# Windowed attention in an encoder layer: scores and attended values as three fp32r products of high and low parts, in place of plain fp32 products

## The chip, the core and the metric

The kernel runs on one core of a Trainium2 chip. The metric is the device time of one execution, in microseconds (us). The engines carry short names in the profile: PE is TensorE (PEld its weight loads), DVE is VectorE, ACT is ScalarE, POOL is GpSimd, and SP is SyncE, which issues most of the DMAs.

## What is computed

One encoder layer over 256 tokens of width 2048: a SwiGLU feed-forward block, a mixer with two groups of heads beside each other, and a second SwiGLU block, each between RMS norms. The mixer projects the tokens once, to 6656 columns; 5120 of them feed eight heads of a bidirectional gated recurrence (HGRN2), the other 1536 feed windowed attention with eight query heads and two key/value heads of width 128. Of the reference, the attention is what matters here (shortened; with 256 tokens every query block sees both key blocks):

```python
def window_attention(q, k, v, sink, rel_table):
    scores = jnp.einsum('bncxgd,bnsxd->bxgncs', qb, kb).astype(jnp.float32) / math.sqrt(ATTN_HEAD_DIM)
    bias = rel_table.astype(jnp.float32)[t5_buckets(rel)]
    scores = jnp.where(valid, scores + bias, NEG_INF)
    probs = jax.nn.softmax(jnp.concatenate([scores, sink_col], axis=-1), axis=-1)[..., :KEY_SPAN]
    out = jnp.einsum('bxgncs,bnsxd->bncxgd', probs.astype(v.dtype), vb)
    return out.reshape(b_, l_, ATTN_WIDTH)
```

All inputs and outputs are float32.

## The kernel before

**Two ways to multiply.** Tiles of type F32R hold float32 numbers that TensorE takes in its reduced form (fp32r). The large projections use them: `split_act` (L176) lets ACT copy a tile into an F32R tile `h` (the high part) and DVE subtract that from the source into `l` (the low part), and each product is then made of high times high, high times low and low times high (L375 to L377, L454; in L322 and L327 the first two stand in one product of 512 columns). Small products, among them those of the recurrence and of the attention, use plain F32 tiles: one `matmul` each.

**The mixer.** The kernel first finishes the first feed-forward block, then works through the columns of `w_mix_in`. `headpair` (L1627) projects 256 columns, which is one pair of heads: per half of the 2048 rows it plays 16 products of 512 columns (L322) and 16 of 256 columns (L327). `proj_N_pieces` does the same for groups of 512 columns (L375 to L377). The loop over `hp` at L1930 takes four head pairs; each projects two forget gates `zf` and `zb`, the recurrence's query `q` and the attention's query `qa`.

**The side list.** Everything that isn't a projection is written as a generator and put into the list `side`: the turned keys (L1660), the recurrence's heads (L1732), their gate (L1802) and the attention (L1833). After each piece of a projection (four products in `headpair`, three in `proj_N_pieces`) `side_step` may play the next part of the first generator; the number that a generator yields is how many pieces pass before its next part. So the side's products stand between the projection's products on PE, and the number is the time that ACT and DVE get to prepare their operands. `LAG_PT` (L1680) is the one between the turned probabilities and their product with the values. A scheduler then orders what each engine was given, engine by engine.

**The attention of one head pair.** Four F32 products `qa` x `kT` of 256 columns make the scores of two heads (L1846); DVE adds the bias (L1854) and the softmax follows. After `LAG_SOFTMAX` pieces PE turns the probabilities `sc` (L1900, eight transposes into two banks), ACT copies each bank into the F32 tile `pt` with every 128 columns reversed (L1903), and after `LAG_PT` pieces four F32 products `va` x `pt` of 256 columns make the attended values `av` (L1911), which are then split into `ya` for the output projection. `va` is written at L1657, `kT` at L1668, `qa` with reversed columns at L1638.

**Rooms.** `mid` holds the mixer's own tiles, one buffer a tag as a rule; `keepy` holds `yt0` to `yt7`, the eight split inputs of the output projection. `yt0` to `yt3` are written by `gated` (L1815), `yt4` to `yt7` by the attention (L1918), one for each head pair.

## Time and profile before

| What | us |
|---|---|
| median of three runs | 1821.24 (1820.77 to 1821.73) |
| the profiled execution's own time | 1822.32 |
| its span, first to last instruction | 1820.5 |
| PE busy in the span | 1807.6 |
| mixer's head pairs and attention, from the first product L322 to the output projection | about 772 to 1033 |

The profile is one execution. Busy time of PE counts pipelined products from start to modelled end, and neighbours overlap; so the step from one product's start to the next is what a product costs in a stream, and an idle time of PE in a row is less than what the stream lost there. In the view of instructions in order of time, a row gives its start, the time from the first start to the last end, engine, line, operation and count; a bracket gives idle time before it and what ended it. An F32 product stands in the trace as two records: L1846 and L1911 have 16 products each and 32 records each.

### The profile page before, as it was taken

Reading aid. Unit: us, or ns where it says so; the run is one execution under the profiler, and the core shown is the slowest. Engines: PE = TensorE matmul, PEld = TensorE weight load, DVE = VectorE, ACT = ScalarE, POOL = GpSimd, SP = SyncE. Lnnn points to the kernel's source line nnn. Section 1 sums busy time; section 2 is a strip of 40 time slices with the busy share of each in tenths; the row PEclk is TensorE's granted clock in tenths of the full one; section 3 lists DMA queues with packets and bytes.
Section 4 is the critical chain, followed back from the end, with each engine's and each line's share of the span. In section 5 each row is a group of like instructions: output and inputs, shape, how many; then the busy total and the mean of one; then the engine's idle time right before and its main releaser. Section 6 shows DMA issues by size and latency. Waiting matters only on the chain.

```text
span 1820.5 us, 23469 instructions
## 1 busy us (share of the span) xinstructions
PE 1807.6 (99%) x8420; PEld 1501.9 (82%) x8420; DVE 1604.3 (88%) x2075; ACT 1137.0 (62%) x1508; POOL 162.9 (9%) x155
## 2 busy tenths in 40 slices
PE   9999999999999999999999999999999999999998
PEld 7888888888888888888888888888888888888886
DVE  7999999999989989477687798899999999999987
ACT  7565666666666657476587556656666666566663
POOL 1011111111011100000000000101111111011110
PEclk9999999999999999999999999999999999999999
DMA  8889999998699995655554456889999998699894
GB/s 302 236 238 285 276 283 256 249 265 249 218 342 271 294 307 189 199 180 176 165 174 149 164 208 239 253 246 265 281 276 267 256 249 249 193 345 302 265 317 157
DMA packets 212196, 447.59 MB, mean 246 GB/s; under 512 B 11768, under 2 KB 46928, under 8 KB 211312
## 3 DMA queue, kind: packets, MB, share of 16 engines
q1 hardware_dynamic: 180000, 384.87, 61.0%
q0 software_dynamic: 31904, 60.96, 19.5%
q8 instruction: 66, 1.08, 0.2%
q14 instruction: 50, 0.41, 0.1%
q10 hardware_dynamic: 176, 0.27, 0.0%
HBM read 433.46 MB, written 12.60 MB: 245 GB/s over the span
## 4 chain that ended last, share of the span: by engine, by line
PE 94%; DVE 2%; ACT 2%; DMA 1%; issue 1%; POOL 0%; DVEq 0%; ACTq 0%; POOLq 0%; SPq 0%
PE pa L454 41%; PE pb L454 35%; PE pa L322 5%; PE pa L327 3%; PE pa L377 2%; PE pa L375 2%; PE pa L376 2%; DMA raw<-in_w_ffn_gate_up_dram 1%; DVE l L178 1%; PE pa L1161 1%; PE pb L1161 1%; ACT h L177 0%; PE pb L1768 0%; PE pb L1742 0%; PE pb L1846 0%
## 5 line engine op out<-in xcount | busy, mean ns | idle before, releaser
L177 ACT CAST h<-raw 128x1024 fp32r<-128x1024 f32 (+1 forms) x867 | 855.1, 1013 | 466.8 <-PE pb L454 151.2
L178 DVE TENSOR_TENSOR l<-raw,h 128x1024 fp32r<-128x1024 f32 (+1 forms) x867 | 987.5, 1170 | 133.9 <-ACT h L177 99.7
L454 PE MATMUL pa<-h,xt 128*128 128x512 f32 x1096 | 384.6, 392 | 0.1
L454 PE MATMUL pb<-h,xt 128*128 128x512 f32 x940 | 336.7, 392 | 0.3 <-DVE pb L1218 0.3
L454 PEld LDWEIGHTS pa<-h,xt 128*128 128x128 f32 x1096 | 205.8, 188 | 44.1 <-DVE xt L233 0.6
L454 PE MATMUL pa<-l,xt 128*128 128x512 f32 x548 | 213.9, 390 | 0.0
L454 PEld LDWEIGHTS pb<-h,xt 128*128 128x128 f32 x940 | 176.4, 188 | 42.4 <-DVE pb L1225 3.6
L454 PE MATMUL pb<-l,xt 128*128 128x512 f32 x470 | 183.2, 390 | 0.0
L997 POOL DMA_DIRECT2D raw<-in_w_ffn_gate_up_dram x78 | 94.6, 1212 | 733.1 <-DVE l L178 642.2
L454 PE MATMUL pb<-h,ht 128*128 128x512 f32 x452 | 159.2, 389 | 0.0
L454 PE MATMUL pa<-h,ht 128*128 128x512 f32 x452 | 159.1, 389 | 0.0
L322 PE MATMUL pa<-xt,h 128*128 128x512 f32 x512 | 124.4, 393 | 0.2 <-ACT h L177 0.2
L454 PEld LDWEIGHTS pa<-l,xt 128*128 128x128 f32 x548 | 103.0, 188 | 20.7 <-DVE l L178 0.9
L454 PE MATMUL pa<-h,xs 128*128 128x512 f32 x312 | 111.6, 389 | 0.0
L322 PEld LDWEIGHTS pa<-xt,h 128*128 128x128 f32 x512 | 93.8, 188 | 18.6 <-ACT h L177 0.6
L454 PE MATMUL pb<-h,xs 128*128 128x512 f32 x312 | 108.7, 389 | 0.0
L454 PEld LDWEIGHTS pb<-l,xt 128*128 128x128 f32 x470 | 88.3, 188 | 16.7
L454 PEld LDWEIGHTS pb<-h,ht 128*128 128x128 f32 x452 | 84.9, 188 | 17.5
L454 PEld LDWEIGHTS pa<-h,ht 128*128 128x128 f32 x452 | 84.9, 188 | 17.5
L454 PE MATMUL pa<-l,ht 128*128 128x512 f32 x226 | 87.9, 389 | 0.0
L454 PE MATMUL pb<-l,ht 128*128 128x512 f32 x226 | 87.9, 389 | 0.0
L1303 POOL DMA_DIRECT2D raw<-in_w_ffn_down_dram x38 | 46.0, 1212 | 371.5 <-DVE la L178 311.3
(297 smaller groups left out, 2575.0 us busy)
## 6 DMA issues: line engine op xcount, KB each, us to landing
raw<-in_w_ffn_gate_up_dram SPq DMA_DIRECT2D x350, 512.0 KB, 5.7
raw<-in_w_ffn_down_dram SPq DMA_DIRECT2D x88, 1024.0 KB, 8.0
raw<-in_w_mix_in_dram SPq DMA_DIRECT2D x52, 1024.0 KB, 5.0
raw<-in_w_ffn_gate_up_dram POOLq DMA_DIRECT2D x78, 512.0 KB, 8.2
raw<-in_w_ffn_down_dram POOLq DMA_DIRECT2D x38, 512.0 KB, 10.1
raw<-in_w_mix_out_dram SPq DMA_DIRECT2D x16, 1024.0 KB, 4.9
ht<-away SPq DMA_DIRECT2D x24, 512.0 KB, 10.4
away<-ht SPq DMA_DIRECT2D x16, 512.0 KB, 6.9
```

Of the source, the lines that this page charges most:

```text
L177: nc.scalar.copy(hi, src)
L178: nc.vector.tensor_tensor(lo, src, hi.bitcast(F32), ALU.subtract)
L322: nc.tensor.matmul(slot[f], weights(hs, kk, f), xcol(xt, k), start=(k == 0), stop=(k == KT - 1))
L327: nc.tensor.matmul(slot[f][:, 0:T], weights(ls, kk, f), xcol(xt, kh * 8 + kk, 0), start=False, stop=False,)
L375: nc.tensor.matmul(dst, xh, h[:, o : o + n], start=(k == 0), stop=False)
L376: nc.tensor.matmul(dst, xh, l[:, o : o + n], start=False, stop=False)
L377: nc.tensor.matmul(dst, xl, h[:, o : o + n], start=False, stop=(k == KT - 1))
L454: nc.tensor.matmul(self.bank(at), lhs, rhs, start=(n == 1), stop=n in (ends, self.of[at]), skip_group_check=n > ends,)
L997: nc.gpsimd.dma_start(raw[:, 0:1024].rearrange("p (k c) -> p k c", k=2), self.source(u, g)[:, :, 1], accum_op=ALU.add,)
L1161: nc.tensor.transpose(bank[:, o : o + P], zs[m][:, k * P : (k + 1) * P], ident)
L1303: nc.gpsimd.dma_start(raws[i][:, 0:1024].rearrange("p (k c) -> p k c", k=2), Pairs.part(w_dn, u, r)[:, :, 512:1024], accum_op=ALU.add,)
```

## The change

Keys, values, queries and probabilities of the attention get a high part of type F32R and a low part, and each F32 product becomes three F32R products, high x high, high x low, low x high, into the same columns of the bank (`thrice`). In detail:

- `va` and `kT` are F32R; their low parts lie in one new tile `low` with the tag `yt2`: for the values one DVE instruction per block of tokens, for the keys `split_act` in place of the copy at L1668.
- `headpair(..., backwards=True)` ends with `split_act` of `y`: a new ACT copy into `qh` (a new tag in `mid`) and a new DVE subtraction into `ql` (tag `yt7`).
- `pt` is F32R, written by the same ACT copy, and DVE subtracts it from the bank into `pl` (tag `yt3`), once for each of two banks.
- `LAG_PT` goes from 4 to 6.

`low`, `ql` and `pl` stand in rooms whose own tiles are written later: `yt2` and `yt3` by the gate of the last two head pairs, `yt7` by the attention of the last.

```diff
@@ -1641,7 +1641,10 @@
                         R.rearrange("p (m c) -> p m c", c=P),
                         ALU.mult,
                     )
-                return y
+                h = mid.tile([P, 2, T], F32R, tag="qh", name=nm("qh"))
+                l = keepy.tile([P, 2, 2, T], F32R, tag="yt7", name=nm("ql"))[:, 0]
+                split_act(h, l, y)
+                return h, l
             nc.vector.tensor_tensor(z, z, bcR(), ALU.mult)
             return z
 
@@ -1650,12 +1653,26 @@
         for i, _ in enumerate(proj_N_pieces(w_in, 6144, 512, xt, sl)):
             if i == 16:
                 spread()
-        va = mid.tile([P, 2, 256], F32, tag="va", name="va")
+        va = mid.tile([P, 2, 256], F32R, tag="va", name="va")
+        low = keepy.tile([P, 2, 2, T], F32R, tag="yt2", name="low")
         kz = mid.tile([P, 2, 256], F32, tag="q", name="kz")
         for m in range(2):
             nc.scalar.mul(kz[:, m, :], sl[m][:, :256], rs2[:, m : m + 1])
-            nc.scalar.mul(va[:, m, :], sl[m][:, 256:], rs2[:, m : m + 1])
-        kT = mid.tile([P, 2, T], F32, tag="kT", name="kT")
+            by = rs2[:, m : m + 1]
+            nc.scalar.mul(va[:, m, :], sl[m][:, 256:], by)
+            nc.vector.scalar_tensor_tensor(
+                low[:, 0, m, :], sl[m][:, 256:], by, va[:, m, :].bitcast(F32), ALU.mult, ALU.subtract
+            )
+        kT = mid.tile([P, 2, T], F32R, tag="kT", name="kT")
+        vas, kTs = (va, low[:, 0]), (kT, low[:, 1])
+
+        def thrice(dst, left, right, first=True, last=True):
+
+            ways = ((0, 0), (0, 1), (1, 0))
+            for i, (a, b) in enumerate(ways):
+                nc.tensor.matmul(
+                    dst, left[a], right[b], start=first and i == 0, stop=last and i == 2
+                )
 
         def turned_keys():
             yield 6
@@ -1665,7 +1682,7 @@
                     nc.tensor.transpose(
                         tp[:, j * T + m * P : j * T + (m + 1) * P], kz[:, m, j * P : (j + 1) * P], ident
                     )
-            nc.scalar.copy(kT.rearrange("p j t -> p (j t)"), tp)
+            split_act(*(t.rearrange("p j t -> p (j t)") for t in kTs), tp)
             yield 1
 
         side.append(turned_keys())
@@ -1677,7 +1694,7 @@
 
         yt = [None] * 8
         ysums = {}
-        LAG_AT, LAG_NORM, LAG_SOFTMAX, LAG_LAST, LAG_PT = 5, 7, 22, 14, 4
+        LAG_AT, LAG_NORM, LAG_SOFTMAX, LAG_LAST, LAG_PT = 5, 7, 22, 14, 6
 
         def hgrn_dir(hp, z, q, d):
 
@@ -1843,12 +1860,10 @@
                     nc.sync.dma_start(bias[:, m, :], windows(later["flat"], off))
                 biases.append(bias)
                 for m in range(2):
-                    nc.tensor.matmul(
+                    thrice(
                         sps[j][:, m * T : (m + 1) * T],
-                        q[:, j, m * P : (m + 1) * P],
-                        kT[:, kv, :],
-                        start=True,
-                        stop=True,
+                        [t[:, j, m * P : (m + 1) * P] for t in q],
+                        [t[:, kv, :] for t in kTs],
                     )
             for j in range(2):
                 nc.vector.scalar_tensor_tensor(
@@ -1891,7 +1906,10 @@
             for i in range(4):
                 nc.vector.tensor_scalar(sc[:, i, :], sc[:, i, :], sm[:, i : i + 1], None, ALU.mult)
             yield LAG_SOFTMAX if hp < 3 else LAG_LAST
-            pt = mid.tile([P, 2, 2, T], F32, tag="sc", name=nm("pt"))
+            pts = (
+                mid.tile([P, 2, 2, T], F32R, tag="sc", name=nm("pt")),
+                keepy.tile([P, 2, 2, T], F32R, tag="yt3", name=nm("pl")),
+            )
             for j in range(2):
                 tps = pb()
                 for sb in range(2):
@@ -1900,20 +1918,20 @@
                         nc.tensor.transpose(
                             tps[:, o : o + P], sc[:, 2 * j + m, sb * P : (sb + 1) * P], ident
                         )
-                nc.scalar.copy(
-                    pt[:, j].rearrange("p s (m c) -> p (s m) c", c=P)[:, :, ::-1],
+                split_act(
+                    *(t[:, j].rearrange("p s (m c) -> p (s m) c", c=P)[:, :, ::-1] for t in pts),
                     tps.rearrange("p (n c) -> p n c", c=P),
                 )
             yield LAG_PT
             av = pb()
             for j in range(2):
                 for sb in range(2):
-                    nc.tensor.matmul(
+                    thrice(
                         av[:, j * T : (j + 1) * T],
-                        va[:, sb, kv * P : (kv + 1) * P],
-                        pt[:, j, sb, :],
-                        start=(sb == 0),
-                        stop=(sb == 1),
+                        [t[:, sb, kv * P : (kv + 1) * P] for t in vas],
+                        [t[:, j, sb, :] for t in pts],
+                        first=sb == 0,
+                        last=sb == 1,
                     )
             t = keepy.tile([P, 2, 2, T], F32R, tag=f"yt{4 + hp}", name=nm("ya"))
             a = av.rearrange("p (j t) -> p j t", j=2)
```

**Order on PE, head pair 1 (counted from 0), attended values.** The rows are PE's products around the attended values while `q` of the next head pair is projected; `pb` is the bank of `av`, `xt` and `h` are the projection's operands. Before:

```order
L322 MATMUL pa_7983<-xt_5939,h_8041 128x512
L1911 MATMUL pb_8057<-pt_8018,va 128x256 x4
L322 MATMUL pa_7982<-xt_5939,h_8045 128x512
L322 MATMUL pa_7983<-xt_5939,h_8045 128x512
L322 MATMUL pa_7982<-xt_5939,h_8045 128x512
L322 MATMUL pa_7983<-xt_5939,h_8045 128x512
L322 MATMUL pa_7982<-xt_5939,h_8045 128x512
L322 MATMUL pa_7983<-xt_5939,h_8045 128x512
L327 MATMUL pa_7982<-xt_5939,l_8042 128x256
L327 MATMUL pa_7983<-xt_5939,l_8042 128x256
```

In the change (L1673 is the `matmul` in `thrice`):

```order
L322 MATMUL pa_8021<-xt_5939,h_8087 128x512
L322 MATMUL pa_8022<-xt_5939,h_8087 128x512
L327 MATMUL pa_8021<-xt_5939,l_8084 128x256
L327 MATMUL pa_8022<-xt_5939,l_8084 128x256
L1673 MATMUL pb_8107<-pt_8057,va 128x256
L1673 MATMUL pb_8107<-pl_8058,va 128x256
L1673 MATMUL pb_8107<-pt_8057,low 128x256
L1673 MATMUL pb_8107<-pt_8057,va 128x256
L1673 MATMUL pb_8107<-pl_8058,va 128x256
L1673 MATMUL pb_8107<-pt_8057,low 128x256
```

Six products of 512 columns and two of 256 (the last four of these eight are shown) now stand ahead of the attended values, which are twelve products in place of four: the two triples shown, and the same two again for the second head of the pair.

**Order on DVE, same place.** `kd` is a factor of the recurrence's next head pair, `k` and `cum` belong to its backward gate. Before:

```order
L1686 TENSOR_SCALAR zb_7974<-zb_7974,oml,lb 128x256 x2
L1714 TENSOR_TENSOR kd_8112<-k_8103,kd_8112 128x512
L1690 TENSOR_SCALAR k_8125<-zb_7974 128x512
L178 TENSOR_TENSOR l_8154<-raw_8147,h_8153 128x1024
L1697 SCALAR_TENSOR_TENSOR cum_8128<-scanm,zb_7974 128x512
```

In the change:

```order
L1703 TENSOR_SCALAR zb_8013<-zb_8013,oml,lb 128x256 x2
L1731 TENSOR_TENSOR kd_8162<-k_8153,kd_8162 128x512
L178 TENSOR_TENSOR pl_8058<-pb_8059,pt_8057 128x4x128
L178 TENSOR_TENSOR pl_8058<-pb_8066,pt_8057 128x4x128
L1707 TENSOR_SCALAR k_8175<-zb_8013 128x512
L178 TENSOR_TENSOR l_8204<-raw_8197,h_8203 128x1024
L178 TENSOR_TENSOR l_8242<-raw_8239,h_8241 128x1024
L1714 SCALAR_TENSOR_TENSOR cum_8178<-scanm,zb_8013 128x512
```

The two subtractions that make `pl` stand behind `kd` and ahead of `k`, two `l` and the scan `cum`.

**Order on ACT, head pair 2, around its attended values.** `zb` is the backward gate of head pair 3, `ya` the copy of the attended values. Before:

```order
L1710 ACT_TABLE_LOAD
L1710 ACTIVATE qd_8624<-dm_8622 128x512
L1712 ACTIVATE kd_8626<-dm_8622 128x512
L1720 ACTIVATE kx_8630<-cum_8620 128x128 x2
L1937 ACT_TABLE_LOAD
L1937 ACTIVATE zb_8507<-zb_8507 128x512
L177 CAST ya_8540<-pb_8535 128x2x256
L1727 ACT_TABLE_LOAD
L1727 ACTIVATE qx_8631<-cum_8620 128x256
L1692 ACT_TABLE_LOAD
L1692 ACTIVATE zb_8507<-zb_8507 128x512
```

In the change:

```order
L1737 ACTIVATE kx_8703<-cum_8693 128x128 x2
L1744 ACTIVATE qx_8704<-cum_8693 128x256
L177 CAST h_8736<-raw_8734 128x1024
L177 CAST h_8740<-raw_8734 128x1024
L1955 ACT_TABLE_LOAD
L1955 ACTIVATE zb_8572<-zb_8572 128x512
L1727 ACT_TABLE_LOAD
L1727 ACTIVATE qd_8697<-dm_8695 128x512
L177 CAST ya_8621<-pb_8608 128x2x256
L1729 ACTIVATE kd_8699<-dm_8695 128x512
L177 CAST h_8778<-raw_8776 128x1024
L177 CAST h_8782<-raw_8776 128x1024
```

Two `h` of the projection stand ahead of the first instruction on `zb` (L1937 before, L1955 in the change) and a third and fourth ahead of the next one (L1692; in the change it comes right after the rows shown), where before there was none in this stretch; the function tables are loaded as often.

## The prediction

> **What bounds the kernel now.** I read the busy times first, then the chain of work that ended last, then PE's own waits in the mixer.
>
> ```profile
> PE 1807.6 (99%) x8420; PEld 1501.9 (82%) x8420; DVE 1604.3 (88%) x2075; ACT 1137.0 (62%) x1508; POOL 162.9 (9%) x155
> ...
> PE 94%; DVE 2%; ACT 2%; DMA 1%; issue 1%; POOL 0%; DVEq 0%; ACTq 0%; POOLq 0%; SPq 0%
> ```
>
> PE is busy for 99% of the span, and 94% of the chain is PE. So a product taken out of PE's stream shortens the kernel by its step, and work on ACT or DVE costs only where PE has to wait for it. The stretches that the change touches (all head pairs, then the surroundings of two attended values), engine by engine:
>
> ```profile
> core 0: us, PE busy (x) PEld busy (x) DVE busy (x) ACT busy (x) POOL busy (x), PEclk, DMA share, GB/s
> 772.00:1035.00 263.00, 261.60 (x1497) 229.94 (x1496) 193.83 (x301) 183.14 (x287) 4.95 (x4) 1.00 0.54 169
> 978.00:993.00 15.00, 15.00 (x82) 12.82 (x80) 9.34 (x16) 14.85 (x23) 0.00 (x0) 1.00 0.22 71
> 921.00:934.00 13.00, 12.16 (x72) 10.55 (x71) 8.57 (x15) 12.47 (x18) 0.00 (x0) 1.00 0.34 112
> ```
>
> DVE has 69 us free of 263 and ACT 80, but in two short stretches ACT is full (14.85 of 15 and 12.47 of 13). PE's waits in the mixer are few:
>
> ```profile
> PE pb L1911 <- ACT pt L1903: 0.8, 1, 0.8
> PE pb L1814 <- DVE on L1804: 0.4, 1, 0.4
> PE pa L322 <- ACT h L177: 0.2, 1, 0.2
> ```
>
> One wait is in front of the attended values, one for an `h`: both in the stretches where ACT is full.
>
> **Term 1: the products.** PE in order of time, around the scores of head pair 0, and around its attended values:
>
> ```profile
> 827.32 1.89 PE L1846 MATMUL pb<-kT,qa 128*128 128x256 f32 x8
> 828.86 0.82 PE L327 MATMUL pa<-xt,l 128*128 128x256 f32 x4
> 829.51 3.34 PE L322 MATMUL pa<-xt,h 128*128 128x512 f32 x14
> 832.70 2.08 PE L327 MATMUL pa<-xt,l 128*128 128x256 f32 x16
> ```
>
> ```profile
> 848.24 1.89 PE L1911 MATMUL pb<-pt,va 128*128 128x256 f32 x8
> 849.77 0.58 PE L375 MATMUL pa<-h,xt 128*128 128x512 f32 x1
> 850.19 0.40 PE L376 MATMUL pa<-l,xt 128*128 128x512 f32 x1
> 850.42 0.39 PE L377 MATMUL pa<-h,xt 128*128 128x512 f32 x1
> ```
>
> ```profile
> L327 PE MATMUL pa<-xt,l x512: 277/283/469, 776.4 to 1002.1; 128*128 128x256 f32 x171
> ```
>
> A product of 256 columns in fp32r is L327: sixteen take 2.08 us from the first start to the last end, one lasts 0.28, so the step is (2.08 - 0.28) / 15 = 0.120 us. One of 512 columns (L322) steps by (3.34 - 0.39) / 13 = 0.227. The fp32 records step by (1.89 - 0.38) / 7 = 0.216, two to a product. What a group of four fp32 products takes from the stream: the attended values start at 848.24, and the second product behind them at 850.19; less one step of 0.227 that is 1.72 us. (The scores: 829.68, the end of the four L327, less the 0.64 that four take, less 827.32, is 1.72 too.) There are two groups in each of four head pairs: 8 x 1.72 = 13.8 us now. Afterwards each is 12 x 0.120 = 1.44 us, 11.5 in all. **Term 1: -2.3 us.** Its price is that of L327, since the new products have its shape, type and a new weight load each.
>
> Here a rule can be weighed. The fp32 record of 256 columns is 0.216 = 2 x 0.108. The Trainium skill, "FP8 and Floating Point Precision", section "TensorE Precision Notes", has a true fp32 product go through the array four times, for the four pairs of high and low halves. By it three of four passes stay, 10.35 us of 13.8, and the term would be -3.45. The trace agrees on four passes of 0.108; but L327, one pass by that rule, steps by 0.120, and I take the row.
>
> **Term 2: the wait before the attended values of head pair 1.**
>
> ```profile
> 929.23 2.00 PE L322 MATMUL pa<-xt,h 128*128 128x512 f32 x8
> 932.07 1.99 PE L1911 MATMUL pb<-pt,va 128*128 128x256 f32 x8 [0.84 <-ACT pt L1903]
> ```
>
> ```profile
> 929.62 1.28 ACT L1712 ACT_TABLE_LOAD   x1
> 930.91 0.63 ACT L1712 ACTIVATE kd<-dm 128x512 f32<-128x512 f32 x1
> 931.45 1.05 ACT L1903 COPY pt<-pb 128x512 f32<-128x512 f32 x2
> 931.58 0.69 DVE L1714 TENSOR_TENSOR kd<-k,kd 128x512 f32<-128x512 f32 x1 [1.20 <-ACT kd L1712]
> ```
>
> The eight L322 would let the next product start at 931.07; it starts at 932.07, 1.0 us lost, and the block then takes 0.1 longer (1.99 in place of 1.89). With `LAG_PT` at 6, eight products pass first: 6 x 0.227 + 2 x 0.120 = 1.60 us, so the attended values start at 932.67 and `pt`'s first bank is there. What is late next is `pl`. DVE has it behind `kd`, which ends at 932.27. Its price is bounded by subtractions from a bank:
>
> ```profile
> L178 DVE TENSOR_TENSOR ya<-pb,ya 128x512 fp32r<-128x512 f32 x2 | 1.4, 687 | 1.4 <-ACT ya L177 1.4
> ...
> L1821 DVE SCALAR_TENSOR_TENSOR yh<-pb,cols,yh 128x256 fp32r<-128x256 f32 x8 | 3.8, 479 | 0.7 <-ACT yh L1820 0.7
> ```
>
> `ya`'s, of the same size, takes 0.69; L1821 takes 0.48 for half the size, two of them 0.96, the upper end. I take 0.69, the like operation: first `pl` at 932.96, second (its copy ends at 932.50) at 933.65. The block's second product waits from 932.79 to about 933.0, the eighth (due at 933.7) hardly. New wait 0.3, old one 1.1: **term 2: -0.8 us**, between -1.1 (no wait) and 0 (`pl` behind an `l` of 1.2 more).
>
> In the other head pairs nothing waited, and the attended values move back by 1.4 or 1.8 us; head pair 0:
>
> ```profile
> 847.48 1.05 ACT L1903 COPY pt<-pb 128x512 f32<-128x512 f32 x2
> 850.02 1.23 DVE L178 TENSOR_TENSOR l<-raw,h 128x1024 fp32r<-128x1024 f32 x1 [2.91 <-ACT h L177]
> ```
>
> `pt` ended at 848.53 and DVE was idle from 847.1 to 850, so `pl` is done by 849.3, ahead of 848.24 + 1.36 = 849.6.
>
> **Term 3: the wait for `h` at 992.7.**
>
> ```profile
> 990.61 2.46 PE L322 MATMUL pa<-xt,h 128*128 128x512 f32 x10
> 993.28 1.89 PE L322 MATMUL pa<-xt,h 128*128 128x512 f32 x7 [0.21 <-ACT h L177]
> ...
> 992.19 1.98 ACT L177 CAST h<-raw 128x1024 fp32r<-128x1024 f32 x2
> ```
>
> Ten L322 would hand on at 992.88; it goes on at 993.28, and the next seven take 1.89 for 1.75: 0.5 us lost, because ACT had its gates ahead of the `h`. In the new order two `h` stand ahead of the gate's sigmoid and two more ahead of its logarithm, so I take this wait as gone: **-0.5 us**, between -0.5 and 0. The price: the backward gate of the last head pair is later by four `h`, 4 x 1.05 = 4.2 us. Its last factors then come near the last `qx`, and PE comes earlier:
>
> ```profile
> 992.01 0.69 DVE L1714 TENSOR_TENSOR kd<-k,kd 128x512 f32<-128x512 f32 x1 [0.57 <-ACT kd L1712]
> ...
> 1000.73 0.41 DVE L1729 TENSOR_TENSOR qx<-q,qx 128x256 f32<-128x256 f32 x1
> ```
>
> and on PE, the products that need them:
>
> ```profile
> 1003.42 1.05 PE L1742 MATMUL pb<-qd,kd 128*128 128x128 f32 x8
> ```
>
> They began at 1003.42; less the 3 us saved by then, 1000.4. `kd` goes from 992.7 to 996.9, and with the query's instructions queued ahead of it on DVE to about 1000. So a wait of 0 to 1 us may arise; I take **+0.3 us**.
>
> **What stays at nothing.** ACT gets four `qh` (0.6 each by the `pt` copies), DVE four `ql` (0.69), eight `pl`, one low part of the keys and two of the values (0.48 by L1821): 9.9 us on DVE, 2.4 on ACT, beside 69 and 80 free. `ql` stands on DVE ahead of the recurrence's `at`, which PE awaits before it comes to the scores; the tightest place is the last head pair:
>
> ```profile
> 1008.65 0.42 DVE L1758 TENSOR_TENSOR at<-keep 128x256 f32<-128x256 f32 x1
> ```
>
> ```profile
> 1009.51 0.72 PE L1768 MATMUL pb<-vh,at 128*128 128x128 f32 x5
> ```
>
> The second head's `at` ended at 1009.07, and its products come eight records of about 0.11 after 1009.51, at 1010.4: 1.3 us of cover for the 0.69 of `ql`, which then hides; without cover it would cost 0.69 in each of four head pairs. No DMA is added or moved. `low`, `ql` and `pl` are last read by the attention of the last head pair, before the tiles that take their rooms are written; that adds no wait.
>
> **Sum.** -2.3 - 0.8 - 0.5 + 0.3 = -3.3 us. The profiled execution took 1822.32 us (span 1820.5), so 1819.0; the median of the runs is 1.1 lower, 1821.24, so **1817.9 us**. About 0.2%, 3.64 us, is what a measurement of this kernel can tell from no change; the forecast lies just inside, with the limit at 1817.6.
>
> **Rivals.**
> - *A product costs one pass.* The new products step by 0.108, half an fp32 record, as a pass of an fp32 record does: 96 x 0.108 = 10.4, term 1 is -3.4, the sum -4.4: 1816.8 (to 1815.9 if no new wait arises). For it: the array takes 256 columns in that time. Against: a record has one weight load for two passes, while L327 has one for each product and steps by 0.120. By the Trainium skill's rule of four passes it would come out here. 18%.
> - *The waits come back.* DVE's low parts or the gate's factors are late, by one `l` (1.2) at one or two places: terms 2 and 3 bring nothing or cost up to 1, the sum is -2.3 to -0.3: 1818.9 to 1820.9. For it: ACT is full there, and DVE does what it gets in order. 20%.
> - *Slower: three products into the same columns hold each other up.* L327 alternates between two banks, the triple does not. If each waits for the one before, the bound is the step of 512 columns, 0.227: 96 x 0.227 = 21.8, 8.0 more than now: 1829. It decides from 0.144 (13.8 / 96), and costs over 0.2% from 0.182. Against: L375 to L377 go three in a row into one bank, and L376 to L377 is 0.23 (850.19, 850.42), no more than L322 while alternating. 5%.
> - *The new products run as fp32 after all*, two records each: 96 x 0.43 = 41.3, 1849. Against: L327, with tiles of the same type, has one record to a product (512 for 512). 1%.
>
> **How the numbers follow.** The forecast, -2.6 to -4.2, gets 56%: 1817.0 to 1818.6, with somewhat under half of it beyond the limit. With the first rival that makes faster by over 0.2%: 0.24 + 0.18 = 0.42; within: 0.32 + 0.20 = 0.52; slower 0.06. The range takes in the first two rivals and the bounds of the waits, 1815.5 to 1821.0.
>
> **What would show it.** Right: 96 records of the new products at 0.12, eight blocks of 1.4 us; no idle time of 0.8 before the attended values of head pair 1; the wait for `h` near 992 gone; PE's sum in the mixer shorter by 3 us and all later stages as long as before. Wrong: steps far from 0.12; a wait of PE on `pl` or `ql` over 0.5 us; a wait at the last L1742 over 1 us.

## The result, and the profile after

| | before | after |
|---|---|---|
| median, measured beside each other, us | 1821.57 | 1819.3 |
| the profiled execution's own time, us | 1822.32 | 1819.29 |
| its span, us | 1820.5 | 1817.5 |
| PE in the chain that ended last | 94% | 92% |

The ratio of the times is 0.9986, with a 95% interval from 0.998 to 0.9993: 2.3 us shorter, within the 0.2% that the forecast called the likelier case, and 1.4 us above the 1817.9 that it named. The busy times and the chain of the changed kernel, from its page:

```profile
PE 1804.9 (99%) x8452; PEld 1500.4 (83%) x8452; DVE 1612.6 (89%) x2090; ACT 1140.1 (63%) x1512; POOL 162.0 (9%) x155
...
PE 92%; DVE 4%; ACT 2%; DMA 1%; issue 1%; POOL 0%; DVEq 0%; ACTq 0%; POOLq 0%
```

PE has 32 more records, 96 for 64, and is busy for 2.7 us less. DVE has the 15 new instructions and 8.3 us more. DVE's share of the chain went from 2% to 4%, so the chain runs through DVE for longer than before. PE's waits in the mixer say where PE now waits for it (engine, result, line, who ended it: sum, times, longest; the lines of the changed kernel lie up to 18 further down, so L1785 is L1768 of before and L1831 is L1814):

```profile
PE pb L1785 <- DVE at L1775: 0.7, 1, 0.7
PE pb L1831 <- DVE on L1821: 0.4, 1, 0.4
```

The waits for `pt` (0.8) and for `h` (0.2) are gone, the one for `on` is as before, and there is a new one of 0.7: the recurrence's products wait for `at`, in head pair 2.

**Reading differences of a tenth.** The times scatter by more than the pieces of this change are worth, the positions within the trace do not. For every projection product that both kernels have, take its start in the one profiled execution less its start in the other. Where nothing differs, this number stays the same to 0.05 us, mostly to 0.03; where it steps, the step is what the kernel gained (minus) or lost there. The steps for `after`, and for the kernels of the experiments:

| kernel | scores of hp 0 | attended values of hp 0 | of hp 1, with their wait | `l` near 944 | `at` of hp 2 | `h` at 992.7 | start of the output projection | mixer, 772 to 1042 | medians |
|---|---|---|---|---|---|---|---|---|---|
| after | -0.29 | -0.30 | -1.21 | +0.28 | +0.97 | -0.51 | +0.20 | **-2.34** | -2.27 |
| e1_scores_only | -0.29 | +0.03 | -0.01 | 0.00 | +0.01 | +0.01 | 0.00 | **-1.09** | -1.09 |
| e2_values_only | 0.00 | -0.30 | -1.21 | +0.28 | +0.29 | -0.51 | +0.24 | **-1.82** | -1.25 |
| e3_lag_only | 0.00 | +0.01 | -1.14 | -0.03 | 0.00 | +0.03 | +0.20 | **-0.96** | -0.92 |
| e5_lag4 | -0.29 | +0.29 | +0.19 | 0.00 | +0.01 | -0.51 | 0.00 | **-1.77** | -1.33 |
| e7_two_products | -0.77 | -0.78 | -1.54 | +0.66 | +0.98 | -0.51 | +0.02 | **-5.83** | |
| e4_q_split_late | -0.29 | -0.30 | -1.22 | +0.26 | +0.37 | -0.51 | +0.20 | **-2.97** | -3.00 |
| e6_ql_pool | -0.29 | -0.30 | -1.20 | +0.26 | +0.29 | -0.51 | +0.20 | **-3.03** | -3.24 |
| e9_kd_pool | -0.29 | -0.30 | -1.20 | -0.03 | +0.66 | -0.51 | +0.20 | **-2.93** | -3.49 |
| e8_lag_at6 | -0.27 | -0.30 | -1.32 | -0.03 | (+4.7, `kd`) | -0.51 | +0.21 | **+0.99** | +0.53 |
| e10_pool_at6 | -0.27 | -0.30 | -1.29 | -0.03 | +0.02 | -0.51 | +0.20 | **-3.67** | -3.47 |
| e11_two_lags | -0.29 | -0.30 | -1.22 | +0.28 | +0.02 | -0.51 | 0.00 | **-3.57** | -3.53 |
| e12_all_three | -0.27 | -0.30 | -1.31 | -0.03 | +0.02 | -0.51 | +0.02 | **-3.89** | -4.66 |

(The attended values of head pairs 2 and 3 and the scores of 1 to 3 step like those of head pair 0, to 0.03; in e5 those of head pairs 2 and 3 step by -0.31. The scores of head pair 2 are taken out of the column for `at`. Where a lag moves a group past a projection piece, the two steps of +1.4 and -1.7 that this makes are added up. "Medians" is the difference of the medians in that comparison, with an interval of about 1.6 us either way, 1.2 for the first row and 2 for the last; the mixer's steps agree with it to 0.8.) In the profiled execution of `after` the code ahead of 772 us, which the change doesn't touch, came out 1.1 us shorter and the code behind 1042 us 0.4 longer than in that of before; so the profiled pair's 3.03 is not the change, and the mixer's 2.34 is.

**The products** came out as forecast. PE in order of time around the scores of head pair 0, after:

```profile
826.23 0.28 PE L1673 MATMUL pb<-kT,qh 128*128 128x256 f32 x1
826.35 0.28 PE L1673 MATMUL pb<-low,qh 128*128 128x256 f32 x1
826.47 0.28 PE L1673 MATMUL pb<-kT,ql 128*128 128x256 f32 x1
826.59 0.28 PE L1673 MATMUL pb<-kT,qh 128*128 128x256 f32 x1
...
827.54 0.28 PE L1673 MATMUL pb<-kT,ql 128*128 128x256 f32 x1
827.66 0.63 PE L327 MATMUL pa<-xt,l 128*128 128x256 f32 x4
```

Twelve records from 826.23 to 827.66 are 1.43 us, a step of 0.119; the four plain products had taken 1.72. Three products into the same columns follow each other like L327's into two banks.

**The attended values of head pair 1**, after:

```profile
929.49 1.06 ACT L177 CAST pt<-pb 128x512 fp32r<-128x512 f32 x2
929.62 0.69 DVE L1731 TENSOR_TENSOR kd<-k,kd 128x512 f32<-128x512 f32 x1 [1.20 <-ACT kd L1729]
930.23 1.28 DVE L178 TENSOR_TENSOR pl<-pb,pt 128x512 fp32r<-128x512 f32 x2
...
930.71 0.28 PE L1673 MATMUL pb<-pt,va 128*128 128x256 f32 x1
...
930.97 0.39 PE L1673 MATMUL pb<-pl,va 128*128 128x256 f32 x1
```

`pt` is there in time, `pl` stands behind `kd` on DVE, and the second product comes 0.26 behind the first in place of 0.12: the small wait for `pl` that term 2 had, 0.14 where it had 0.3.

**The new wait**, DVE and PE of head pair 2, after, and below them the same place before:

```profile
950.70 1.23 DVE L178 TENSOR_TENSOR l<-raw,h 128x1024 fp32r<-128x1024 f32 x1 [0.45 <-ACT h L177]
951.84 0.68 DVE L178 TENSOR_TENSOR ql<-qa,qh 128x512 fp32r<-128x512 f32 x1
952.45 1.35 DVE L1768 COPY_PREDICATED keep<-tri,pb 128x512 f32<-128x512 uint8 x2
953.70 0.74 DVE L1775 TENSOR_TENSOR at<-keep 128x256 f32<-128x256 f32 x2
...
954.16 2.05 PE L1785 MATMUL pb<-vh,at 128*128 128x128 f32 x16 [0.72 <-DVE at L1775]
```

```profile
952.92 1.34 DVE L1751 COPY_PREDICATED keep<-tri,pb 128x512 f32<-128x512 uint8 x2
954.16 0.74 DVE L1758 TENSOR_TENSOR at<-keep 128x256 f32<-128x256 f32 x2
...
956.17 1.95 PE L1768 MATMUL pb<-vh,at 128*128 128x128 f32 x16
```

Before, the first of the two `at` (they start 0.33 apart) was done at 954.57, 1.6 us ahead of PE. Afterwards PE would have come at 953.2, the 954.16 less the 0.97 lost: 3.0 earlier, 1.1 of it from ahead of 772, so 1.9 by the change. `at` comes 0.46 earlier, which is 0.65 later against the same 1.1: that is `ql`. 1.9 + 0.65 - 1.6 is the 0.95 that PE loses. The first bracket shows a second thing: DVE stood idle for 0.45 in front of its `l`, waiting for an `h` of ACT. Point 4 of the account below comes back to it.

### The profile page after: what moved, and what is told of

Same layout as the page of the kernel before. It is cut to its first block, busy times and chain, and to the rows that moved or that the text cites. A ratio compares the mean times of both kernels' runs of the same rounds, so it can differ in the third digit from the quotient of the medians.

```text
span 1817.5 us, 23552 instructions
## 1 busy us (share of the span) xinstructions
PE 1804.9 (99%) x8452; PEld 1500.4 (83%) x8452; DVE 1612.6 (89%) x2090; ACT 1140.1 (63%) x1512; POOL 162.0 (9%) x155
## 4 chain that ended last, share of the span: by engine, by line
PE 92%; DVE 4%; ACT 2%; DMA 1%; issue 1%; POOL 0%; DVEq 0%; ACTq 0%; POOLq 0%
PE pa L454 40%; PE pb L454 35%; PE pa L322 5%; PE pa L327 3%; PE pa L377 2%; PE pa L376 2%; PE pa L375 2%; DVE l L178 2%; DMA raw<-in_w_ffn_down_dram 1%; ACT h L177 1%; PE pb L1673 1%; PE pa L1161 1%; PE pb L1161 1%; PE pb L1785 0%; PE pb L1759 0%
```

## The experiments

My theory of the shortfall: the products brought what was forecast, and what is missing went at three places where PE now comes too early for another engine, the largest of them where `ql` stands ahead of `at`. The rival: PE is merely earlier everywhere and meets `at` as it was, so `ql` has no part in it and moving it brings nothing. The runs take the parts one by one.

**One half alone.** e1_scores_only keeps the scores' three products and leaves attended values and `LAG_PT` as before; e2_values_only keeps the attended values' and the lag of 6, with plain scores. The diffs show the products and the lag only; the operands of the half that is left out are plain F32 tiles again.

```diff
 e1_scores_only, against the change
-        LAG_AT, LAG_NORM, LAG_SOFTMAX, LAG_LAST, LAG_PT = 5, 7, 22, 14, 6
+        LAG_AT, LAG_NORM, LAG_SOFTMAX, LAG_LAST, LAG_PT = 5, 7, 22, 14, 4
...
-                    thrice(
+                    nc.tensor.matmul(
                         av[:, j * T : (j + 1) * T],
-                        [t[:, sb, kv * P : (kv + 1) * P] for t in vas],
-                        [t[:, j, sb, :] for t in pts],
+                        va[:, sb, kv * P : (kv + 1) * P],
+                        pt[:, j, sb, :],
 e2_values_only, against the change
-                    thrice(
+                    nc.tensor.matmul(
                         sps[j][:, m * T : (m + 1) * T],
-                        [t[:, j, m * P : (m + 1) * P] for t in q],
-                        [t[:, kv, :] for t in kTs],
+                        q[:, j, m * P : (m + 1) * P],
+                        kT[:, kv, :],
```

> Before, with only the scores as three products (queries and keys split; values, probabilities and the lag of 4 as before). Theory: four groups at -0.30 are -1.2 us; the wait of 1.0 before the attended values of head pair 1 stays, since nothing about it changed; the wait for `h` near 992 stays or goes by the order on ACT (0 or -0.5); `ql` ahead of `at` costs 0 to 0.5, because PE is not yet early there. Together -0.7 to -1.7, about 1820.4. Rival (`ql` alone makes the wait of about 1.0 in head pair 2): -0.2 to -0.7.

> Before, with only the attended values as three products (values and probabilities split, the lag at 6; queries and keys as before). Theory: four groups at -0.31 are -1.2 us, the wait before the attended values of head pair 1 goes (-0.9), the wait for `h` near 992 goes (-0.5), an `l` behind `pl` may cost 0.3, and there is no wait on `at`, since `ql` is absent: -2.3 to -2.8, so about as much as the whole change. Rival (`pl` is what puts DVE behind): the wait on `at` in head pair 2 appears here too, 0.5 or more, and the sum is -1.3 to -1.9.

e1 is 1.09 us shorter by the medians (ratio 0.9996, 0.9987 to 1.0005), e2 1.25 (0.9993, 0.9984 to 1.0002): each alone is too little for the times. In the positions e1 has just the scores' four steps, none of the losses, and both old waits. e2 has the attended values' steps, both waits gone, and without any `ql` still 0.28 at `l` and 0.29 at `at`. Its mixer is 1.82 shorter, less than the 2.3 to 2.8 that was expected. So `ql` is 0.6 to 0.7 of the 0.97 lost there, and 0.3 is there without it.

**The lag and the products apart.** e3_lag_only is the kernel before with `LAG_PT` 6; e5_lag4 is the change with `LAG_PT` 4.

```diff
 e3_lag_only, against before
-        LAG_AT, LAG_NORM, LAG_SOFTMAX, LAG_LAST, LAG_PT = 5, 7, 22, 14, 4
+        LAG_AT, LAG_NORM, LAG_SOFTMAX, LAG_LAST, LAG_PT = 5, 7, 22, 14, 6
 e5_lag4, against the change
-        LAG_AT, LAG_NORM, LAG_SOFTMAX, LAG_LAST, LAG_PT = 5, 7, 22, 14, 6
+        LAG_AT, LAG_NORM, LAG_SOFTMAX, LAG_LAST, LAG_PT = 5, 7, 22, 14, 4
```

> The kernel before with LAG_PT 6 in place of 4 and nothing else; all products stay plain fp32. Theory A (the later place alone removes the two waits, the products in parts have no share in that): by the positions of the projections' products, attended values of head pair 1 -0.9 us, the wait for h near 992.7 -0.5, the other groups of scores and attended values 0.00, so -1.4 in the mixer and 1820.0 as the median. Rival B (the h wait went because PE came earlier, by the products saved before it): only the -0.9, and 0.0 at 992.7. For the three small losses of the change, 0.28 before L327's l at 944, 0.98 before at in head pair 2, 0.20 at the output projection's start: theory A expects the part that comes from PE arriving earlier at the unchanged DVE queue, 0.2 to 0.3 at 944 and 0 to 0.3 at at; nothing of the 0.20 if that comes from pl or the products.

> The change with LAG_PT back at 4: products in parts, attended values at their old place. The first pt is there at about 931.9 in the clock of before; pl stands behind kd on DVE, which ends at 932.3, so theory A expects the wait of 0.9 back and 0.3 to 0.7 more for pl: attended values of head pair 1 between 0.0 and +0.5 us in place of -1.21; the h wait at 992.7 stays (0.0 in place of -0.5); the products' gain the same, eight times -0.30. The loss at at in head pair 2 shrinks from 0.98, since PE is then about 1.2 us later there and ql has more cover: 0 to 0.4. Sum in the mixer -1.2 to -2.2 in place of -2.34. Rival (the two places of lag are worth nothing with products in parts): the mixer as in the change, within 0.2.

e3: 1820.69 us against 1821.61 (ratio 0.9996, 0.9987 to 1.0005). The wait of head pair 1 goes by the lag alone, -1.14; the change's -0.9 is that less `pl`. The wait for `h` at 992.7 stays, against theory A, and nothing is lost at `l` or `at`, where it expected up to 0.3 each. e5: 1820.28 (0.9993, 0.9984 to 1.0002); the wait of head pair 1 is back, and waits for `pl` are added to it and in head pair 0, as the view of PE's waits in e5 shows:

```profile
PE pb L1673 <- ACT pt L177: 0.8, 1, 0.8
PE pb L1673 <- DVE pl L178: 0.5, 2, 0.3
```

but the `h` wait is gone there too, which was not expected. It isn't PE's earlier coming either: at 990 PE is further ahead in e3, which waits, than in e5, which doesn't. What differs is ACT's order. ACT in e3, with PE below it, then ACT in e5:

```profile
986.06 0.63 ACT L1692 ACTIVATE zb<-zb 128x512 f32<-128x512 f32 x1
986.60 1.04 ACT L177 CAST h<-raw 128x1024 fp32r<-128x1024 f32 x1
...
990.38 0.61 ACT L1712 ACTIVATE kd<-dm 128x512 f32<-128x512 f32 x1
990.90 2.93 ACT L177 CAST h<-raw 128x1024 fp32r<-128x1024 f32 x3
...
991.98 2.11 PE L322 MATMUL pa<-xt,h 128*128 128x512 f32 x8 [0.23 <-ACT h L177]
```

```profile
985.71 1.99 ACT L177 CAST h<-raw 128x1024 fp32r<-128x1024 f32 x2
987.72 1.28 ACT L1709 ACT_TABLE_LOAD   x1
```

In e3, as before, one `h` stands ahead of a block of gate functions and the next behind it; in e5 and in the change two stand ahead of the gate's logarithm. That order comes with the attended values in parts (e2, e5, all later kernels), not with the lag. Two losses are sorted as well: e5 loses nothing at `at`, where PE comes 2.0 us later (the steps up to 937 add up to -0.1 there, to -2.1 in the change), nor at `l`, where DVE has one `l` further ahead again; and nothing at the output projection.

**`ql` out of `at`'s way.** e4_q_split_late splits the query behind the two `at`; e6_ql_pool leaves it in place but gives the subtraction to POOL.

```diff
 e4_q_split_late
-                split_act(h, l, y)
-                return h, l
+                return h, l, y
 ...
                 ats.append(at)
+            split_act(*qa)
             yield LAG_AT
 ...
 e6_ql_pool
-                split_act(h, l, y)
+                nc.scalar.copy(h, y)
+                nc.gpsimd.tensor_tensor(l, y, h.bitcast(F32), ALU.subtract)
```

> The change, with the query's split put behind the recurrence's two `at` of the same head pair; by the order of instructions only DVE's `ql` moves, from ahead of the masked copies to behind the last or ahead of the last `at`. Theory (the wait of 0.98 us before L1785 in head pair 2 is `ql`'s 0.68 queued ahead of `at` on a DVE that is behind): the wait goes or shrinks below 0.4, the scores do not wait for `ql`, the other steps of the stream stay; 0.7 to 1.0 us less than the change, about 1818.4. Rival (DVE is late there because of `pl` and the `l` before it, whatever stands directly ahead of `at`): the wait stays at 0.6 or more, at most 0.3 us less than the change.

> The change, with `ql` subtracted on POOL in place of DVE (four instructions). Theory (DVE's 0.68 is what delays `at`): the wait before L1785 in head pair 2 shrinks as in the run with the late split, 0.7 to 1.0 us less than the change, as long as POOL ends `ql` within the 4 us before the scores. Rival (DVE late for other reasons): at most 0.3 less. If POOL takes over 4 us for it, a wait before the scores appears and the run is slower than the change by up to 4 x that excess.

e4: 1818.45 us against 1821.45 (ratio 0.9985, 0.9976 to 0.9993); e6: 1818.21 (0.9985, 0.9976 to 0.9994). Both give back 0.6 to 0.7 at `at` and leave everything else where it was. The times alone can't tell either from the change, whose ratio is 0.9986; the positions can. The view of PE's waits lists only the old one for `on` in the mixer of either. So the rival falls, but for the 0.3 that stays: that much PE is too early for `at` itself, as the sum of 1.9 and 1.6 above has it.

**The price of one product.** e7_two_products leaves out the third product of each triple, the low part of the left operand (queries, values) times the high part of the other; that part of the computation isn't done.

```diff
-            ways = ((0, 0), (0, 1), (1, 0))
+            ways = ((0, 0), (0, 1))
 ...
```

> The change without its third product: the product of the right operand's high part (keys, softmax transposed by name) with the other's low part is left out, so 64 products in place of 96, and that part of the computation is not done. It prices one product where it stands. Theory (L327's step holds in a triple): each of the eight groups is shorter by 4 x 0.12 = 0.48 us, so scores of head pair 0 -0.77 against before in place of -0.29, attended values of head pair 0 -0.78. Rival (a pass of 0.108): 0.43 a group, -0.72. Rival (the last product of a triple hides part of its step behind the next weight load): less than 0.40 a group. Waits near the attended values and at may grow by as much as PE comes earlier.

Seven of the eight groups are shorter by 0.46 to 0.48 us, for four products fewer: 0.12 each, L327's step, and not 0.108. The attended values of head pair 1 are shorter by 0.33, in a block in which PE waits for `pl` in both kernels. The earlier PE loses 0.66 in place of 0.28 at `l`.

**DVE's queue ahead of `l`.** e9_kd_pool is e6 with one product of the gates in head pair 2 on POOL; e8_lag_at6 has `LAG_AT` 6 besides.

```diff
+            side_engine = nc.gpsimd if hp == 2 and d == 1 else nc.vector
-            nc.vector.tensor_tensor(kd, k.rearrange("p j t -> p (j t)"), kd, ALU.mult)
+            side_engine.tensor_tensor(kd, k.rearrange("p j t -> p (j t)"), kd, ALU.mult)
 e8_lag_at6 also
-        LAG_AT, LAG_NORM, LAG_SOFTMAX, LAG_LAST, LAG_PT = 5, 7, 22, 14, 6
+        LAG_AT, LAG_NORM, LAG_SOFTMAX, LAG_LAST, LAG_PT = 6, 7, 22, 14, 6
```

> The change with ql on POOL and, in head pair 2 alone, the backward direction's product for kd on POOL too (kd is wanted by PE some 6 us later). It takes 0.60 us from DVE's queue ahead of the l at 943.2. Theory (the 0.28 lost at 944 is DVE's queue of nine instructions from the gates ahead of that l): the 0.26 at 944 goes to 0.0, the rest as with ql on POOL alone, mixer -3.3 in place of -3.03. Rival 1 (the l waits for its h from ACT or its piece of x): 0.26 stays. Rival 2 (a POOL product takes 1.8 us or more and DVE is slowed beside it): kd late, PE waits before L1760 by 0.2 to 1 us.

> As the kernel with kd and ql on POOL, and LAG_AT 6 in place of 5, so that one more item of the projections stands between the products for the scores of the recurrence and those on at. Theory (what is left of the loss before at in head pair 2, 0.3 us, is at itself being late by that much): it goes to 0, and with it the mixer comes to -3.5 to -3.7, the sum of all gains with no new wait; median 1817.7 to 1818.0. Rival (the later place moves other work of that chain, the normalization and the output rows, and a wait appears at another place): no gain over LAG_AT 5, with a wait of 0.3 us or more elsewhere in the mixer.

e9: 1818.12 us against 1821.61 (ratio 0.9982, 0.9974 to 0.9991). The loss at `l` is gone, but `at` loses 0.37 more, so the mixer gains nothing over e6: PE is earlier, and `at` is no earlier. Nor was DVE's queue relieved. In the view of POOL and DVE, POOL's product lies beside an `l` that takes 2.33 us, where `l` takes 1.21 elsewhere:

```profile
940.00 1.49 POOL L1733 TENSOR_TENSOR kd<-k,kd 128x512 f32<-128x512 f32 x1 [35.85 <-ACT kd L1730]
```

```profile
939.63 0.69 DVE L1649 TENSOR_TENSOR q<-q,R 128x512 f32<-128x512 f32 x1
940.23 2.33 DVE L178 TENSOR_TENSOR l<-raw,h 128x1024 fp32r<-128x1024 f32 x1
...
950.24 1.21 DVE L178 TENSOR_TENSOR l<-raw,h 128x1024 fp32r<-128x1024 f32 x1
```

What helped at 944 was the order, which puts an `l` ahead of four of the gates' products. e8 was the miss: 1822.14 us (ratio 1.0002, 0.9993 to 1.0011). The second rival, a slow POOL, happened there and larger than it said:

```profile
944.45 6.70 POOL L1733 TENSOR_TENSOR kd<-k,kd 128x512 f32<-128x512 f32 x1 [37.82 <-ACT kd L1730]
```

```profile
944.13 0.42 DVE L1748 TENSOR_TENSOR qx<-q,qx 128x256 f32<-128x256 f32 x1
944.47 0.68 DVE L1731 TENSOR_TENSOR qd<-q,qd 128x512 f32<-128x512 f32 x1
945.07 0.41 DVE L1748 TENSOR_TENSOR qx<-q,qx 128x256 f32<-128x256 f32 x1
945.41 4.62 DVE L178 TENSOR_TENSOR l<-raw,h 128x1024 fp32r<-128x1024 f32 x4
949.95 0.74 DVE L919 TENSOR_TENSOR qa<-pa,qa 128x256 f32<-128x256 f32 x2
950.61 1.16 DVE L1638 TENSOR_TENSOR qa<-qa,R 128x256 f32<-128x256 f32 x2
```

```profile
951.21 1.22 PE L1761 MATMUL pb<-qd,kd 128*128 128x128 f32 x6 [2.79 <-POOL kd L1733]
```

POOL's product ends 1.2 us after DVE comes to its first instruction that reads a bank, and in that time DVE's next pair with two inputs in SBUF (where all tiles lie but the banks `pa` and `pb`), L1638, takes 1.16 us, where it takes 0.74 in the kernel before.

**The lags alone.** e10_pool_at6 is e8 with `kd` back on DVE (e6 with `LAG_AT` 6); e11_two_lags is e4 with two lags changed in one head pair each; e12_all_three is e10 with the last head pair's `LAG_PT` at 4.

```diff
 e10_pool_at6, against e6
-        LAG_AT, LAG_NORM, LAG_SOFTMAX, LAG_LAST, LAG_PT = 5, 7, 22, 14, 6
+        LAG_AT, LAG_NORM, LAG_SOFTMAX, LAG_LAST, LAG_PT = 6, 7, 22, 14, 6
 e12_all_three, against e10
-            yield LAG_PT
+            yield LAG_PT if hp < 3 else 4
 e11_two_lags, against e4
-            yield LAG_AT
+            yield LAG_AT + (hp == 2)
-            yield LAG_PT
+            yield LAG_PT if hp < 3 else 4
```

> The change with ql on POOL and LAG_AT 6 in place of 5; kd is on DVE again. With kd on POOL the same lag had no wait for at, but one of 2.8 us for kd: POOL's product for it lay from 944.45 to 951.15 while DVE ran products of two tiles in SBUF one behind the other. Theory (that wait came from kd's place on POOL and not from the lag): no wait before L1760, none before at; scores and at of head pair 2 -0.3 net of the moved group; 0.26 for l near 944 may stay or go with DVE's order; mixer -3.3 to -3.7; median 1817.7 to 1818.2. Rival (the lag itself brings the wait): a wait of 1 us or more before L1760 or another product of head pair 2, and the mixer above -2.7.

> The change with ql split behind the two at on DVE (no work on POOL), LAG_AT 6 in head pair 2 alone, and LAG_PT 4 in the last head pair alone, 6 in the others. Theory (three of the change's losses are places in the queue: 0.20 at the output projection's start comes from LAG_PT 6 in the last head pair; 0.3 to 0.4 at at in head pair 2 from at being late; 0.26 at 944 from DVE): the 0.20 goes to 0.0, the loss at at to 0.0, 0.26 stays: mixer -2.97 - 0.20 - 0.36 = -3.5, and the last head pair's attended values stay at -0.31 with no wait for pl. Median 1817.8 to 1818.2. Rival (a wait for pl or pt comes in the last head pair with lag 4, or the h wait at 992.7 comes back with the moved group): mixer above -3.0.

> The change with ql on POOL, LAG_AT 6 in all head pairs, and LAG_PT 4 in the last head pair alone. Theory (the losses are places in queues and add up): the mixer at -3.67 - 0.20 = -3.9, with 0.00 at the output projection's start, -0.03 at 944 and no wait before at; median 1817.6 to 1817.9. Rival (the 0.20 is an accident of when PE arrives, not of the lag): it is still there, or another loss of that size is, and the mixer stays at -3.6 to -3.7.

All three came out as their theory had it: mixer -3.67, -3.57 and -3.89. e10: 1817.98 us against 1821.45 (ratio 0.9979, 0.997 to 0.9988); e11: 1817.92 (0.998, 0.9972 to 0.9989); e12: 1817.43 against 1822.09 (0.9973, 0.9962 to 0.9985). By the mixer's steps e12 is the shortest that does the whole computation; its median lies 0.2 below what was expected, and the intervals of the three overlap. In its mixer the view of PE's waits has one line left, which was there before the change:

```profile
PE pb L1832 <- DVE on L1822: 0.4, 1, 0.4
```

e12 also shows what the 0.20 at the output projection is. The transposes of `on` in the changed kernel, then in e12:

```profile
1032.96 1.23 PE L1831 MATMUL pb<-ident,on 128*128 128x128 f32 x8
```

```profile
1032.73 0.60 PE L1832 MATMUL pb<-ident,on 128*128 128x128 f32 x4
1033.08 0.48 PE L454 MATMUL pa<-l,yh 128*128 128x512 f32 x1
1033.40 0.60 PE L1832 MATMUL pb<-ident,on 128*128 128x128 f32 x4
```

With lag 6 in the last head pair the eight transposes stand together, and the second four have no projection product in front of them while DVE finishes the second `on`; with lag 4, as before the change, one stands between. It is this order that counts, and not the lag as such: e7 has lag 6 too, there one projection product stands between (1030.01, between the transposes from 1029.65 and those from 1030.32), and it loses 0.02.

## Why the prediction was right in sign and short in size

1. *Term 1, -2.3:* right. The eight groups step by -0.29 to -0.33, -2.47 in all. The rival of one pass fell with e7: 0.12 a product. The Trainium skill, "FP8 and Floating Point Precision", section "TensorE Precision Notes", has four passes through the array for a true fp32 product. By an estimate from it three of four would stay, 75%; the trace has 1.43 of 1.72 us, 83%, so passes alone don't price the new products here. What the trace shows of a plain product is two records of 0.216 us; the four passes of 0.108 that the prediction read in it are a division, which no row shows. The rival of same-column products holding each other up fell by the rows.
2. *Term 2, -0.8:* right, -0.9. e3 separates it: -1.14 for the later place, and 0.2 back with the products in parts, 0.14 of it the wait for `pl` in the rows.
3. *Term 3, -0.5:* right, -0.51, and by the reason given, ACT's order; e3 and e5 rule out the lag. The +0.3 for a wait at the last L1742 did not come; that it brought the forecast nearer to the result is luck, since what was lost was lost elsewhere.
4. *"What stays at nothing":* **this is the step that failed.** It said that `ql` hides, with the last head pair as the tightest place, 1.3 us of cover. In the last head pair it did hide. In head pair 2 `at` was late and 0.97 us was lost, 0.6 to 0.7 of it `ql`'s (e4, e6). The cover there was larger, 1.6 us by the rows of before, but it was not there any more. The forecast's own terms took some 2 us out of PE's stream ahead of that place (four groups of 0.29 and 0.8), and where DVE doesn't follow, PE's earlier coming eats the cover. That DVE was full there the trace of before shows, in a stretch that the forecast didn't ask for, because it had looked for full stretches around waits only:

```profile
939.00:954.00 15.00, 15.00 (x95) 13.46 (x94) 14.93 (x25) 9.84 (x18) 0.00 (x0) 1.00 0.81 212
```

   DVE is busy for 14.93 of 15 us (the third pair of columns) up to the very `at` in question. `ql`, queued ahead of that `at`, takes 0.68 and put it back by 0.65. Why the rest of the queue didn't come earlier with PE is another matter, and the row of the changed kernel with the 0.45 shows it. Up to the product for `qa` (L1638, which ends at 950.25; before at 951.86) DVE is 0.5 earlier, the 1.1 from ahead of 772 taken off. Then it waits for `h`. `l`, the next transfer of weights and that `h`, before and after:

```profile
941.69 1.21 DVE L178 TENSOR_TENSOR l<-raw,h 128x1024 fp32r<-128x1024 f32 x1
942.97 0.38 SPq L153 DMA_DIRECT2D raw<-in_w_mix_in_dram  x1
...
949.53 1.05 ACT L177 CAST h<-raw 128x1024 fp32r<-128x1024 f32 x1
```

```profile
943.15 5.76 DVE L178 TENSOR_TENSOR l<-raw,h 128x1024 fp32r<-128x1024 f32 x5
944.40 0.38 SPq L153 DMA_DIRECT2D raw<-in_w_mix_in_dram  x1
...
949.62 1.05 ACT L177 CAST h<-raw 128x1024 fp32r<-128x1024 f32 x1 [3.05 <-DVE qa L919]
```

   In both the transfer is issued as the first `l` shown ends (at 942.90 before and near 944.4 in the change; in e9, where that `l` ends at 942.56, it is issued at 942.59). In the change this `l` stands behind six products for the recurrence's operands (`q`, `kd`, `qd`, `qx`) that it stood ahead of before; with the 1.1 added, `l` is 2.6 later, the transfer 2.5 and `h` 1.2. (The bracket names DVE's `qa`, which ended at the same time; in e2 and e6, with the same order, it names the transfer.) So `at` would have been as late as before without `ql`: in e4 it starts at 952.40, and that trace is 1.77 early at 772, which makes 954.17 against 954.16. That this wait holds the 0.3 that is left in e2, e4 and e6 is read from the rows; no run takes it out alone.
5. *Two smaller losses, neither of them in the forecast:* 0.28 at `l` near 944, that same `l`. The kernels in which all five `l` of this stretch stand behind those products (after, e2, e4, e6, e7, e11) lose 0.26 or more there; where one of the five stands further ahead, nothing is lost. And 0.20 at the output projection, which comes with `LAG_PT` 6 in the last head pair wherever the eight transposes then stand together.

The sum: -2.47 - 0.9 - 0.51 is -3.9; the three losses are +1.45; a tenth is left over. That makes -2.34 where -3.3 was said. The rival "the waits come back" was the nearest of those named: its mechanism (DVE's low parts late, in the order of its queue) and its bound (1818.9 and above) hold, though not at the places that it named and not by one `l`. e12, with the losses out, has -3.89: the gains were all there.

## What to carry to other kernels

When an edit takes time out of the engine that bounds the kernel, every cover downstream shrinks by what was taken out ahead of it, except where the other engines move forward with it; so ask for each engine's busy share in short stretches over the whole changed part, not just around today's waits, and take nothing queued in a stretch with no gap as hidden. Look as well at what the new order does to the instructions that set transfers going: here an `l` that moved back by 2.6 us held its transfer back by 2.5. Put new work behind what the bounding engine will ask for next, not ahead of it. Differences too small for the times can be read from the positions of unchanged instructions in two traces.

## What the runs showed of the hardware

- **POOL and DVE held each other up.** A product of two tiles in SBUF, 128x512, took POOL 1.49 us in e9, and 6.70 in e8, where DVE ran seven instructions with both inputs in SBUF without a gap; and an `l` on DVE that came 0.23 us behind POOL's product in e9 took 2.33 in place of 1.21. The Trainium skill, "SBUF — State Buffer", section "Who interferes with whom", says that a DVE instruction with two inputs in SBUF contends with a POOL instruction that reads SBUF, and calls the shared pair of ports an exclusive lock. The rows agree in both directions: in e9 `l` is long beside POOL's product, in e8 POOL's product ends only after DVE has come to an instruction that reads a bank. In both runs POOL's product began while DVE was in an instruction with two inputs in SBUF (L1649 in e9, the first L1748 in e8); why POOL came next behind that one in e9, and only behind six more in e8, no run shows.
- The step of 256 columns in fp32r is 0.119 to 0.12 us whether products alternate between two banks (L327) or go three times into the same columns (L1673).
- Between two traces, the distance of two products in an unchanged stretch of the mixer repeats to 0.05 us over 50 us and more. The scatter of the traced times lies in other stages: ahead of 772 us they are from 1.8 us shorter to 0.4 longer than in the trace of before, behind 1042 us from 0.1 shorter to 1.1 longer.
